# A trunk block on one core: block sums on token rows, and the MLP's second product in two groups of eight pairs

## The chip, the cores and the metric

The kernel runs on one core of a Trainium2 chip. The metric is the device time of one execution in microseconds. Before the change the median of three runs is 1608.74 us (1605.66 to 1609.58).

## The reference

One layer on 1024 frames of width 1024, all in float32: a mixing step (a convolution and a recurrent branch), a cross-attention into 256 memory tokens, and an MLP, each with a norm ahead and a residual add behind. The change concerns the end of the attention and the MLP:

```
hf = rmsnorm(x, g_ffn)                              # x: 1024 x 1024
x = x + square(relu(hf @ w_ff1)) @ w_ff2            # w_ff1: 1024 x 4096, w_ff2: 4096 x 1024
return rmsnorm(x, g_final)
```

## The kernel before, in words

**Precision.** Each float32 operand of a matmul is split into two parts, hi (a cast on ScalarE, L70) and lo (the value less hi, L71, on VectorE or, where a call says so, on GpSimd). A product is three matmuls: hi by hi, hi by lo, lo by hi (`mm3`, L79 to L81), added up in one PSUM bank of 128x512.

**Seven products instead of eight.** Both matrix products of the MLP are done on 2x2 blocks with seven block products and sums of blocks ahead and behind (j = 1 to 7). For `hf @ w_ff1` the token side is cut into two halves of 512 tokens and two halves of 512 features; the sums of these blocks are made once, in `blocks` (L1190), row block by row block (128 tokens). Row blocks 0 to 3 belong to the first token half and give b1 and b2 alone. Row blocks 4 to 7 give the other five, b3 to b7: the normed rows are transposed on TensorE, and sums are taken out of PSUM on VectorE and GpSimd.

**Up (the first product).** `up` (L1319) runs over 16 pairs of 128 columns of `w_ff1`, seven block products of 12 matmuls each. `up_operands` loads a pair's weights (L1290) and splits them, a pair ahead. A result is squared after relu on ScalarE (L1337, L1338), and the seven sums that the second product needs on its left are stored to `da` in memory (L1332), all from SyncE's queue; four of the seven come from sums on GpSimd.

**Down (the second product).** For each pair and j, a 128x512 left operand comes back from `da` (L1434) and a right one is a block, or a difference of blocks, of two rows of `w_ff2` (L1397, 512 KB a load). Before, the pairs stand in four groups of four. For a group and a j, four row blocks i are worked off one after the other: one bank, 12 matmuls for the four pairs, one drain into `acc[j, i]` (ScalarE copy L1454 in the first group, VectorE add L1456 later). The operands of the next j are prepared while this j runs, one pair per row block: the right lo part on VectorE, the left one on GpSimd (`down_operands`, L1400). Ahead of the first group's second row block 16 residual loads from `dx` are issued (`residual`, L1384). In the last group `merge` (L1461) adds the seven results up, half of them on VectorE and half on GpSimd, and `finish_rows` (L1486) does the final norm.

**What sets the order.** Each engine works off its own queue in order. A scheduler sets that order when the program is built, by a priority that is the place in the code (`self.at(p, ...)` gives code the priority of another place) and by an estimate of when inputs are ready. Waits between engines are semaphores, set by the data. Buffers are rings of a fixed number of tiles; a new use of a tile waits for the last reader of the old one. SyncE issues all loads and stores; an issue that waits holds up all behind it.

Of the kernel before, what the change touches and what calls it, by code (L numbers as in the profile page):

```python
# [25 lines left out]
GROUP = 4  # L26
GROUPS = PAIRS // GROUP
TAPS = 31
# [21 lines left out]
class Trunk:  # L50
# [189 lines left out]
    def norm(self, pool, src, g):  # L240
        t, r = self.rms_scale(pool, src)
        self.nc.vector.scalar_tensor_tensor(t, src, r, g, ALU.mult, ALU.mult)
        return t
# [25 lines left out]
    def run(self):  # L269
# [13 lines left out]
        with ctx:  # L283
# [46 lines left out]
            x1 = [px1.tile([P, D], F32, name=f"x1_{i}") for i in range(8)]  # L330
# [45 lines left out]
            B, feed = self.attention(pT, pQ, pG, pn, h1, x1, ahead, swap)  # L376
            early = tc.cur_priority
# [3 lines left out]
            self.mlp([push(right, n) for n in ("pE", "pF", "pS")], pn, B, early, lambda: (pop(left, 2), push(left, "pD"))[1])  # L381
            pop(right, 4)
# [697 lines left out]
    def attention(self, pT, pQ, pG, pn, h1, x1, ahead, swap):  # L1080
# [65 lines left out]
        def feed():  # L1146
            i, t = norms.pop(0)
            self.blocks(pT, t, i, B)
# [20 lines left out]
        return B, feed  # L1169
# [20 lines left out]
    def blocks(self, pool, t, i, B):  # L1190
# [4 lines left out]
        def turned(k):  # L1195
            pp = self.bank(self.ps, "mm")
            for j in range(4):
                nc.tensor.transpose(pp[:, j * P : (j + 1) * P], t[:, (k + j) * P : (k + j + 1) * P], self.ident)
            return pp.rearrange("p (k t) -> p k t", t=P)

        def at(p):
            return [z[:, :, ts_] for z in B[p]]

        def tmp():
            return pool.tile([P, 2, M], F32, tag="pe", name="tc", bufs=4).rearrange("p a (k t) -> p (a k) t", t=P)

        if i < 4:
            for p, k in ((1, 0), (2, 4)):
                self.split(*at(p), turned(k))
            return  # L1210
        pp = turned(0)
        b12 = tmp()
        nc.scalar.copy(b12, pp)
        hi, lo = at(1)
        t1 = tmp()
        nc.vector.tensor_tensor(t1, pp, f32(hi), ALU.subtract)
        nc.gpsimd.tensor_tensor(t1, t1, f32(lo), ALU.subtract)
        pp = turned(4)
        t2 = tmp()
        nc.vector.tensor_tensor(t2, pp, t1, ALU.subtract)  # L1220
        self.split(*at(6), t2)
        nc.vector.tensor_tensor(b12, pp, b12, ALU.subtract)
        self.split(*at(7), b12)
        self.split(*at(5), t1, nc.gpsimd)
        self.split(*at(3), pp)
        hi, lo = at(2)
        t4 = tmp()
        nc.vector.tensor_tensor(t4, f32(hi), t2, ALU.subtract)
        nc.gpsimd.tensor_tensor(t4, t4, f32(lo), ALU.add)
        self.split(*at(4), t4, nc.gpsimd)  # L1230
# [5 lines left out]
    def mlp(self, pools, pn, B, early, deeper):  # L1236
        (self.pE, self.pF, self.pS), self.pn = pools, pn
# [4 lines left out]
        def first():  # L1242
            for p in range(2):
                next(made[p])
                next(made[p])

        self.at(early, first)
# [5 lines left out]
        for u in ups:  # L1253
            for _ in u:
                pass
        self.down_tiles(deeper())
        stages = [(g, j) for g in range(GROUPS - 1) for j in (1, 5, 6, 7, 4, 2, 3)]
        stages += [(GROUPS - 1, j) for j in (1, 6, 7, 5, 4, 2, 3)]
        made = [[], []]
        for _ in self.down_operands(*stages[0], *made):  # L1260
            pass
        for n, (g, j) in enumerate(stages):
            now, made = made, [[], []]
            ahead = self.down_operands(*stages[n + 1], *made) if n + 1 < len(stages) else iter(())
            self.down(g, j, *now, ahead)
# [4 lines left out]
    def ring_of(self, *tags):  # L1270
        return itertools.cycle(
            [lambda a=a: a[0].tile(a[1], a[2], tag=a[3], name=a[3], bufs=a[4]) for a in tags for _ in range(a[4])]
        )

    def up_tiles(self):

        wide = [P, 2, HALF]
        self.operands = (self.pE, wide, F32R, "s", 6), (self.pS, wide, F32R, "s", 3)
        self.rows_of = (self.pm, [P, D], F32, "ms", 2), (self.pE, [P, D], F32, "w", 2)
        self.sring = self.ring_of(*self.operands)  # L1280

    def up_operands(self, p, out):
# [3 lines left out]
        for k in range(2):  # L1286
            pool, tag = ((self.pm, "ms"), (self.pE, "w"))[k]
            w = pool.tile([P, 4, 256], F32, tag=tag, name="w1", bufs=2)
# [30 lines left out]
    def up(self, p, A, B, ahead):  # L1319
# [11 lines left out]
        def put(j, z):  # L1331
            nc.sync.dma_start(self.da[j - 1, p], z)  # L1332
# [14 lines left out]
        c11 = put(1, act(product(2), p1))  # L1347
# [6 lines left out]
        c22 = put(4, act(pp, u3))  # L1354
# [4 lines left out]
        c21 = put(2, act(product(4), u3))  # L1359
        put(3, pooled(s2, c21, s2, ALU.subtract))  # L1360

    def down_tiles(self, pD):
# [16 lines left out]
        own = (pD, [P, 2, HALF], F32R, "r", 7), (pD, [P, D], F32, "w2", 8)  # L1379
        self.sring, self.wring = self.ring_of(own[0], *self.operands), self.ring_of(*self.rows_of, own[1])  # L1380
        self.rows = {}
        self.sums = lambda: sums(*((j, i) for j in (1, 5, 6, 7, 4, 2, 3) for i in range(4) if (j, i) not in self.acc))

    def residual(self):  # L1384

        nc, acc = self.nc, self.acc
        nc.sync.dma_start(self.gfin, self.a["g_final"].rearrange("(o d) -> o d", o=1).broadcast_to([P, D]))
        for j, o, c in ((5, 4, HALF), (4, 4, 0), (2, 0, 0), (3, 0, HALF)):
            for i in range(4):
                nc.sync.dma_start(acc[j, i], self.dx[i + o, :, c : c + HALF])  # L1390
        for i in range(4):
            self.both(acc[3, i], acc[3, i], acc[5, i], ALU.subtract, nc.gpsimd)

    def row(self, g, e, q):
        t = next(self.wring)()
        f = 2 * (g * GROUP + q) + e
        self.nc.sync.dma_start(t, self.a["w_ff2"][0, f * P : (f + 1) * P, :])  # L1397
        return t

    def down_operands(self, g, j, left, right):  # L1400

        nc, rows = self.nc, self.rows
        if (g, 0) not in rows:
            rows[g, 0] = [self.row(g, 0, q) for q in range(GROUP)]
        if j == 3 and g < GROUPS - 1:
            rows[g + 1, 0] = [self.row(g + 1, 0, q) for q in range(GROUP)]
        for q in range(GROUP):
            b11, b12 = (rows[g, 0][q][:, n * HALF : n * HALF + HALF] for n in range(2))
            if j not in (1, 5) or g == GROUPS - 1 and j == 5:
                b21, b22 = (rows[g, 1][q][:, n * HALF : n * HALF + HALF] for n in range(2))  # L1410
            if j == 1:
                t = b11
            elif j == 4:
                t = self.both(b11, b21, b11, ALU.subtract)
            elif j in (2, 3):
                t = b21 if j == 2 else b22
            elif g < GROUPS - 1:

                if j == 5:
                    t = self.both(b11, b12, b11, ALU.subtract)  # L1420
                elif j == 6:
                    t = self.both(b11, b22, b11, ALU.subtract)
                else:
                    t = self.both(b12, b22, b12, ALU.subtract)
            elif j == 6:

                self.both(b12, b22, b12, ALU.subtract)
                t = self.both(b11, b12, b11, ALU.add)
            elif j == 7:
                t = b12  # L1430
            else:
                t = self.both(b12, b22, b11, ALU.subtract)
            st = self.py_tile(F32)
            nc.sync.dma_start(st, self.da[j - 1, g * GROUP + q])  # L1434
            for out, src, eng in ((right, t, nc.vector), (left, st, nc.gpsimd)):
                z = next(self.sring)()
                self.split(z[:, 0], z[:, 1], src, eng)
                out.append((z[:, 0], z[:, 1]))
            if j == 1 and q == GROUP - 1:
                rows[g, 1] = [self.row(g, 1, q) for q in range(GROUP)]  # L1440
            yield

    def down(self, g, j, left, right, ahead):
        nc = self.nc
        for i in range(4):
            pp = self.bank(self.ps, "mm")
            ts_ = slice(i * P, i * P + P)
# [76 lines left out]
```

## Time and profile before

| | |
|---|---|
| median of 3 runs | 1608.74 us (1605.66 to 1609.58) |
| profiled execution | 1608.75 us, of it span 1607.0 us |
| TensorE busy | 1504.7 us, 94% |
| VectorE, ScalarE, GpSimd busy | 1225.4, 657.3, 676.6 us |
| bytes moved | 201.15 MB, mean 125 GB/s |
| granted TensorE clock, mean | 0.965 |

The span runs from the first to the last instruction of the profiled execution. "Busy" is the time in which an engine had an instruction of its own to work on; "PEclk" is the clock that TensorE was granted, 1.00 for 2.4 GHz and 0.50 for 1.2 GHz, as a mean over a stretch. In rows, `out<-in` names the tiles without their numbers, `xN` counts instructions, and a bracket at the end is how long the engine stood idle ahead of the row and what released it. All up to about 900 us (mixing, attention's queries and scores) is the same in both kernels. The up runs from about 939 to 1259 us, the down from 1266 us on.

### The profile page before, as it was taken

How to read it: one execution, taken by the hardware profiler on the slowest of the kernel's cores; microseconds unless marked ns; L12 is line 12 of the kernel's file. 1: busy time of each engine (PE TensorE's matmuls, PEld its weight loads, DVE VectorE, ACT ScalarE, POOL GpSimd, SP SyncE). 2: the span in 40 equal slices, each digit the busy share in tenths (PEclk: the TensorE clock that was granted, in tenths of full speed). 3: DMA queues.
4: the chain of work that ended last, by engine and by line, in shares of the span. 5: the costliest groups of instructions: out<-in, count | busy, mean ns of one | idle time of the engine just before them, and what ended most of it. 6: DMA issues, size and time to landing. Idle time of an engine off the chain costs nothing.

```text
span 1607.0 us, 22127 instructions
## 1 busy us (share of the span) xinstructions
PE 1504.7 (94%) x8066; PEld 1221.3 (76%) x8066; DVE 1225.4 (76%) x1691; ACT 657.3 (41%) x1219; POOL 676.6 (42%) x529
## 2 busy tenths in 40 slices
PE   6998988999999999999999949999999899999986
PEld 4776766778877778888888738888888678888864
DVE  5979898998888986473554788666655688899997
ACT  5423223223556452343222354555554354344323
POOL 4212337424345451421010075544444485565774
PEclk9999998989999999999999979999999999999997
DMA  7144436354344332231100314544444774544322
GB/s 236 41 152 137 125 105 187 99 165 127 110 126 135 122 119 73 79 98 45 49 14 27 132 39 151 171 144 148 160 151 164 255 269 144 158 146 148 93 59 105
DMA packets 171119, 201.15 MB, mean 125 GB/s; under 512 B 11679, under 2 KB 116439, under 8 KB 171010
## 3 DMA queue, kind: packets, MB, share of 16 engines
q1 hardware_dynamic: 171010, 199.73, 39.5%
q8 instruction: 64, 1.05, 0.3%
q14 instruction: 45, 0.37, 0.1%
HBM read 139.92 MB, written 59.77 MB: 124 GB/s over the span
## 4 chain that ended last, share of the span: by engine, by line
PE 66%; DVE 18%; issue 5%; DMA 5%; POOL 4%; ACT 2%; SPq 1%; DVEq 0%; POOLq 0%; ACTq 0%
DVE acc L617 7%; PE mm L80 5%; PE mm L79 5%; PE mm L81 5%; PE pr L80 5%; PE pr L81 5%; PE pr L79 5%; PE mm L445 3%; PE ep L81 2%; PE cp L81 2%; PE ep L80 2%; PE cp L80 2%; PE cp L79 2%; PE ep L79 2%; PE py L79 2%
## 5 line engine op out<-in xcount | busy, mean ns | idle before, releaser
L617 DVE SCALAR_TENSOR_TENSOR acc<-u,cw,acc 128x1024 f32<-128x1024 f32 (+1 forms) x150 | 205.1, 1367 | 3.8
L263 POOL TENSOR_TENSOR wlo<-wst,whi 128x1024 fp32r<-128x1024 f32 (+2 forms) x34 | 86.5, 2548 | 139.9 <-ACT whi L262 139.7
L71 POOL TENSOR_TENSOR s<-y,s 128x512 fp32r<-128x512 f32 x70 | 115.8, 1679 | 43.4 <-ACT s L70 39.0
L71 DVE TENSOR_TENSOR s<-f,s 128x512 fp32r<-128x512 f32 x48 | 53.3, 1112 | 52.9 <-ACT s L70 52.9
L93 POOL TENSOR_TENSOR rsr<-rsv,mhalf 128x1 f32<-128x1 f32 x34 | 20.1, 590 | 164.8 <-DVE rsv L88 161.1
L70 ACT CAST s<-w 128x512 fp32r<-128x512 f32 x92 | 56.7, 619 | 76.5 <-PE us L81 32.6
L71 POOL TENSOR_TENSOR r<-y,r 128x512 fp32r<-128x512 f32 x42 | 67.9, 1640 | 40.0 <-ACT r L70 40.0
L1337 ACT ACTIVATE y<-y 128x512 f32<-128x512 f32 x64 | 40.4, 632 | 79.6 <-DVE y L1233 72.0
L71 DVE TENSOR_TENSOR s<-w,s 128x512 fp32r<-128x512 f32 x58 | 64.4, 1123 | 10.3 <-ACT s L70 10.3
L1233 POOL TENSOR_TENSOR s<-y 128x512 f32<-128x512 f32 x32 | 41.5, 1317 | 59.8 <-ACT y L1338 59.8
L71 POOL TENSOR_TENSOR s<-w,s 128x512 fp32r<-128x512 f32 x34 | 46.3, 1366 | 37.6 <-ACT s L70 37.6
L445 PE MATMUL mm<-memT,wkv 128*128 128x256 f32 x256 | 61.3, 385 | 0.0
L71 DVE TENSOR_TENSOR r<-w,r 128x512 fp32r<-128x512 f32 x44 | 56.5, 1304 | 3.7 <-ACT r L70 3.7
L881 DVE TENSOR_TENSOR fs<-xt,PL 128x4 f32<-128x4 f32 (+15 forms) x128 | 53.9, 421 | 6.2 <-ACT PL L873 3.4
L262 ACT CAST whi<-wst 128x1024 fp32r<-128x1024 f32 (+2 forms) x34 | 35.0, 1031 | 56.9 <-PE mm L80 15.0
L1069 POOL TENSOR_TENSOR wql<-wst,wqh 128x1024 fp32r<-128x1024 f32 x8 | 20.0, 2495 | 88.6 <-ACT wqh L1068 88.6
L79 PE MATMUL mm<-hT1hi,whi 128*128 128x512 f32 (+1 forms) x120 | 50.9, 425 | 2.6 <-DVE z L501 1.4
L81 PE MATMUL mm<-hT1hi,wlo 128*128 128x512 f32 (+1 forms) x120 | 50.0, 416 | 2.7 <-POOL wlo L263 2.7
L445 PEld LDWEIGHTS mm<-memT,wkv 128*128 128x128 f32 x256 | 46.4, 190 | 6.1
L70 ACT CAST r<-w 128x512 fp32r<-128x512 f32 x44 | 27.2, 618 | 58.0 <-PE cp L81 40.9
L70 ACT CAST s<-f 128x512 fp32r<-128x512 f32 x64 | 38.3, 621 | 28.8 <-DVE f L1233 26.3
L80 PE MATMUL mm<-hT1lo,whi 128*128 128x512 f32 (+1 forms) x120 | 49.4, 411 | 0.0
(1002 smaller groups left out, 5030.6 us busy)
## 6 DMA issues: line engine op xcount, KB each, us to landing
w<-in_w_ff_dram SPq DMA_DIRECT2D x58, 512.0 KB
y<-da SPq DMA_DIRECT2D x112, 256.0 KB
da<-y SPq DMA_DIRECT2D x80, 256.0 KB
wst<-in_w_in_dram SPq DMA_DIRECT2D x32, 512.0 KB
da<-s SPq DMA_DIRECT2D x32, 256.0 KB
dz<-sg SPq DMA_DIRECT2D x24, 256.0 KB
dz<-z SPq DMA_DIRECT2D x24, 256.0 KB
xt<-in_x_dram SPq DMA_DIRECT2D x8, 512.0 KB
```

Source lines behind the costliest of these rows:

```text
L70: nc.scalar.copy(hi, src)
L71: (eng or nc.vector).tensor_tensor(lo, src, f32(hi), ALU.subtract)
L79: nc.tensor.matmul(ps, lh, rh, start=first and k == 0, stop=False)
L80: nc.tensor.matmul(ps, lh, rl, start=False, stop=False)
L81: nc.tensor.matmul(ps, ll, rh, start=False, stop=last and k == n - 1)
L262: nc.scalar.copy(hi, st)
L263: nc.gpsimd.tensor_tensor(lo, st, f32(hi), ALU.subtract)
L445: nc.tensor.matmul(dst, w[:, k, :], mem[k // 4][:, k % 4, :], start=k == 0, stop=k == KC - 1)
L617: nc.vector.scalar_tensor_tensor(acc, u[:, t : t + n], self.cw[:, t * 4 + c : t * 4 + c + 1], acc, ALU.mult, ALU.add)
L881: nc.vector.tensor_tensor(tmp, x, rows, ALU.mult)
L1233: (eng or self.nc.vector).tensor_tensor(out, x, y, op)
L1337: nc.scalar.activation(c, c, AF.Relu)
```

## The change

1. `GROUP` goes from 4 to 8. `down` now works in steps (group, j, pair): a step does its three matmuls on each of four open banks, and all four are drained after eight pairs. The last block (last group, j = 3) is done row block by row block, when all eight operands are there. Operands are prepared six steps ahead (`AHEAD`), the first six at the priority of the last up pair.
2. Rows of `w_ff2` are loaded as two halves of 256 KB, the second row of a pair only when the second j needs it. The residual loads are spread over four j, and the final gain is loaded in the last group.
3. Both lo parts of a step are made on VectorE; all merges on GpSimd. The final norm scales one half row early (`half_row`), and at the end takes one scale on VectorE and one on ScalarE (`rows_out`).
4. `blocks` takes the four sums of a row block on normed token rows (in place: GpSimd for row blocks 4 to 6, VectorE for 7), and then transposes and splits five blocks instead of two. For this the normed rows of blocks 0 to 3 stay in `x1`, and the store of a row to `dx` now stands ahead of its norm.
5. The stores of c11, c22 and c21, three of a pair's seven, go to ScalarE's queue. The rings of weights and operands turn in another order.

The core of the diff (other lines follow from these):

```diff
-GROUP = 4
+GROUP = 8
+AHEAD = 6
...
-                    norms.append((i, self.norm(pn, x1[i], g)))
                     nc.sync.dma_start(self.dx[i], x1[i])
+                    norms.append((i, self.norm(pn, x1[i], g, i < 4)))
...
+        def put(p, src):
             pp = self.bank(self.ps, "mm")
             for j in range(4):
+                nc.tensor.transpose(pp[:, j * P : (j + 1) * P], src[:, j * P : (j + 1) * P], self.ident)
+            hi, lo = (z[:, :, ts_] for z in B[p])
+            self.split(hi, lo, pp.rearrange("p (k t) -> p k t", t=P))
...
+        def less(out, x, y):
+            return self.both(out, x, y, ALU.subtract, nc.vector if i == 7 else nc.gpsimd)
...
+        (b11, b21), (b12, b22), (t1, t2) = (halves(z) for z in (x1[i - 4], t, x1[i]))
+        less(t1, b12, b11)
+        less(t2, b22, t1)
+        put(3, b22)
+        put(5, t1)
+        put(6, t2)
+        put(7, less(b12, b22, b12))
+        put(4, less(b21, b21, t2))
...
+        steps = [(g, j, q) for g in range(GROUPS) for j in ORDER[g] for q in range(GROUP)]
...
+        for n in range(AHEAD):
+            self.at(late, lambda: ahead(n))
+        for n, step in enumerate(steps):
+            ahead(n + AHEAD)
+            self.down(*step, ready)
...
-        c11 = put(1, act(product(2), p1))
+        c11 = put(1, act(product(2), p1), nc.scalar)
...
-        c22 = put(4, act(pp, u3))
+        c22 = put(4, act(pp, u3), nc.scalar)
...
-        c21 = put(2, act(product(4), u3))
+        c21 = put(2, act(product(4), u3), nc.scalar)
...
+    def row(self, g, q, e, n):
...
+        f, cs = 2 * (g * GROUP + q) + e, slice(n * HALF, n * HALF + HALF)
+        self.nc.sync.dma_start(self.rows[g, q, e][:, cs], self.a["w_ff2"][0, f * P : (f + 1) * P, cs])
...
-            for out, src, eng in ((right, t, nc.vector), (left, st, nc.gpsimd)):
...
-                self.split(z[:, 0], z[:, 1], src, eng)
+            self.split(z[:, 0], z[:, 1], src)
...
+            self.open = [self.bank(self.ps, "mm") for _ in range(4)]
...
+        def part(i, q, right, left):
+            ts_ = slice(i * P, i * P + P)
+            self.mm3(self.open[i], [(left[0][:, ts_], left[1][:, ts_])], [right], q == 0, q == GROUP - 1)
...
+        if not (last and j == 3):
+            now = ready.pop(0)
+            for i in range(4):
+                part(i, q, *now)
+        elif q == GROUP - 1:
+            for i in range(4):
+                for k in range(GROUP):
+                    part(i, k, *ready[k])
+                self.drain(g, j, i)
+            return
...
-        eng = nc.vector if i % 2 else nc.gpsimd
...
+            self.both(acc[to, i], acc[to, i], acc[by, i], ALU.add, nc.gpsimd)
```

**Where the order changes.** TensorE, from the last transposes to the first up product; `junk` is a normed row, `x1_k` a row block that the sums were taken in, `b1h` and `b1l` the parts of block 1. Before:

```order
L1198 MATMUL py_7885<-ident_115,junk_7821 128x128 x4
L1198 MATMUL us_7895<-ident_115,junk_7821 128x128 x4
L1198 MATMUL ep_7941<-ident_115,junk_7860 128x128 x4
L1198 MATMUL cp_7951<-ident_115,junk_7860 128x128 x4
L1198 MATMUL mm_7981<-ident_115,junk_7916 128x128 x4
L1198 MATMUL pr_7991<-ident_115,junk_7916 128x128 x4
L1198 MATMUL py_8012<-ident_115,junk_7972 128x128 x4
L1198 MATMUL us_8022<-ident_115,junk_7972 128x128 x4
L79 MATMUL mm_8074<-b1h_7471,s_8058 128x512
L80 MATMUL mm_8074<-b1l_7472,s_8058 128x512
```

After:

```order
L1212 MATMUL pr_7981<-ident_115,x1_1_3392 128x128 x4
L1212 MATMUL ep_7999<-ident_115,junk_7925 128x128 x4
L1212 MATMUL cp_8006<-ident_115,x1_6_3395 128x128 x4
L1212 MATMUL mm_8013<-ident_115,x1_6_3395 128x128 x4
L1212 MATMUL us_8038<-ident_115,junk_7989 128x128 x4
L1212 MATMUL pr_8021<-ident_115,junk_7925 128x128 x4
L1212 MATMUL mm_8045<-ident_115,x1_7_3397 128x128 x4
L1212 MATMUL py_8029<-ident_115,x1_2_3394 128x128 x4
L81 MATMUL mm_8106<-b1h_7471,s_8090 128x512
L82 MATMUL mm_8106<-b1l_7472,s_8090 128x512
L83 MATMUL mm_8106<-b1h_7471,s_8090 128x512
```

The two transposes per row block became five, of rows and of sums, and the first up product stands behind that of `x1_2`, the last sum of row block 6; three transposes of row block 7 follow it.

ScalarE, from the last squares of the up to the first casts of the down (`y` is a result or a loaded left operand, `ms` a row of `w_ff2`, `r` and `s` operands). Before:

```order
L1337 ACTIVATE y_10568<-y_10568 128x512
L1338 ACTIVATE y_10568<-y_10568 128x512
L1337 ACTIVATE y_10591<-y_10591 128x512
L1338 ACTIVATE y_10591<-y_10591 128x512
L70 CAST s_10647<-y_10642 128x512
L70 CAST r_10620<-ms_10610 128x512
L70 CAST r_10623<-y_10618 128x512
L70 CAST r_10628<-ms_10612 128x512
```

After:

```order
L1341 ACTIVATE y_10600<-y_10600 128x512
L1342 ACTIVATE y_10600<-y_10600 128x512
L1341 ACTIVATE y_10623<-y_10623 128x512
L1342 ACTIVATE y_10623<-y_10623 128x512
L1336 DMA da_62<-y_10623 128x512
L72 CAST s_10687<-y_10682 128x512
L72 CAST r_10651<-ms_10647 128x512
L72 CAST r_10654<-y_10649 128x512
L72 CAST r_10662<-ms_10658 128x512
```

The store of the last result (c21 of the last pair) now stands in ScalarE's queue, between its square and the first cast of the down.

GpSimd in the last group (`p60` is `acc[6, 0]`, and so on; `r` and `s` with `L71` are left lo parts). Before:

```order
L71 TENSOR_TENSOR r_12720<-y_12715,r_12720 128x512
L71 TENSOR_TENSOR s_12745<-y_12740,s_12745 128x512
L1233 TENSOR_TENSOR p60_10679<-p60_10679,p10_10671 128x512
L1233 TENSOR_TENSOR p20_10691<-p20_10691,p10_10671 128x512
L1233 TENSOR_TENSOR p62_10681<-p62_10681,p12_10673 128x512
L1233 TENSOR_TENSOR p22_10693<-p22_10693,p12_10673 128x512
L71 TENSOR_TENSOR s_12768<-y_12763,s_12768 128x512
L71 TENSOR_TENSOR s_12791<-y_12786,s_12791 128x512
L71 TENSOR_TENSOR s_12814<-y_12809,s_12814 128x512
L71 TENSOR_TENSOR s_12837<-y_12832,s_12837 128x512
L1233 TENSOR_TENSOR p70_10683<-p70_10683,p60_10679 128x512
L71 TENSOR_TENSOR r_12861<-y_12856,r_12861 128x512
```

After:

```order
L1236 TENSOR_TENSOR p60_10732<-p60_10732,p10_10724 128x512
L1236 TENSOR_TENSOR p20_10744<-p20_10744,p10_10724 128x512
L1236 TENSOR_TENSOR p61_10733<-p61_10733,p11_10725 128x512
L1236 TENSOR_TENSOR p21_10745<-p21_10745,p11_10725 128x512
L1236 TENSOR_TENSOR p62_10734<-p62_10734,p12_10726 128x512
L1236 TENSOR_TENSOR p22_10746<-p22_10746,p12_10726 128x512
L1236 TENSOR_TENSOR p63_10735<-p63_10735,p13_10727 128x512
L1236 TENSOR_TENSOR p23_10747<-p23_10747,p13_10727 128x512
L1236 TENSOR_TENSOR p70_10736<-p70_10736,p60_10732 128x512
L1236 TENSOR_TENSOR p71_10737<-p71_10737,p61_10733 128x512
```

Before, merges stand between lo parts for the next j; now merges stand alone, for all four row blocks, and the lo parts are in VectorE's queue.

## Rows read from the trace of the kernel before

**Rows 1.** The page, busy time and share of TensorE, TensorE's weight loads and the others.
```profile
PE 1504.7 (94%) x8066; PEld 1221.3 (76%) x8066; DVE 1225.4 (76%) x1691; ACT 657.3 (41%) x1219; POOL 676.6 (42%) x529
```

**Rows 2.** Table of stretches: window, length, busy of PE, PEld, DVE, ACT, POOL, clock, DMA share.
```profile
920.00:965.00 45.00, 22.24 (x96) 17.03 (x95) 37.61 (x45) 24.94 (x45) 33.29 (x25) 0.73 0.16 51
...
1000.00:1100.00 100.00, 100.00 (x443) 82.81 (x442) 66.78 (x83) 51.46 (x85) 51.52 (x39) 1.00 0.49 159
...
1245.00:1270.00 25.00, 18.25 (x73) 14.62 (x72) 9.29 (x10) 10.44 (x18) 10.10 (x9) 0.89 0.51 179
1270.00:1290.00 20.00, 15.82 (x65) 12.40 (x64) 14.85 (x18) 5.38 (x11) 9.90 (x8) 0.93 1.03 373
1290.00:1315.00 25.00, 24.29 (x96) 19.46 (x96) 24.81 (x18) 15.61 (x30) 24.57 (x16) 0.89 0.65 222
...
1400.00:1500.00 100.00, 100.00 (x443) 82.81 (x442) 86.27 (x94) 38.43 (x72) 60.08 (x38) 1.00 0.47 140
...
1540.00:1590.00 50.00, 43.73 (x170) 33.12 (x171) 46.87 (x54) 15.50 (x36) 36.47 (x25) 0.93 0.20 64
1590.00:1607.00 17.00, 3.67 (x17) 2.70 (x15) 10.06 (x22) 5.06 (x14) 2.20 (x4) 0.67 0.42 155
```

**Rows 3.** TensorE's timeline: start us, us, engine, line, operation, tiles, count, idle ahead.
```profile
908.57 0.60 PE L1198 MATMUL us<-ident,junk 128*128 128x128 f32 x4
...
962.98 0.79 PE L79 MATMUL py<-b5h,s 128*128 128x512 f32 x1 [12.61 <-ACT s L70]
...
1258.60 0.39 PE L80 MATMUL us<-b4l,s 128*128 128x512 f32 x1
1258.83 0.39 PE L81 MATMUL us<-b4h,s 128*128 128x512 f32 x1
1265.96 0.79 PE L79 MATMUL mm<-r 128*128 128x512 f32 x1 [6.75 <-ACT r L70]
...
1568.57 0.79 PE L81 MATMUL mm<-r 128*128 128x512 f32 x1 [4.06 <-POOL r L71]
...
1593.28 0.39 PE L81 MATMUL us<-s 128*128 128x512 f32 x1
```

**Rows 4.** GpSimd's timeline: two operations of the block sums, one stretch of the last group.
```profile
924.62 2.25 POOL L1217 TENSOR_TENSOR tc<-tc,b1l 128x512 f32<-128x512 f32 x1 [0.25 <-DVE tc L1216]
...
960.41 1.26 POOL L71 TENSOR_TENSOR b4l<-tc,b4h 128x512 fp32r<-128x512 f32 x1 [0.73 <-ACT b4h L70]
...
1566.81 3.39 POOL L71 TENSOR_TENSOR r<-y,r 128x512 fp32r<-128x512 f32 x2
```

**Rows 5.** GpSimd by lines from 920 to 965 us, the powers: busy, mean ns | idle.
```profile
L93 POOL TENSOR_TENSOR rsr<-rsv,mhalf 128x1 f32<-128x1 f32 x4 | 2.6, 660 | 7.4 <-DVE rsv L88 7.4
```

**Rows 6.** VectorE's timeline: norms, operations with GpSimd idle and busy, the end.
```profile
921.14 1.28 DVE L242 SCALAR_TENSOR_TENSOR junk<-x,rsr,g 128x1024 f32<-128x1024 f32 x1
...
933.93 1.60 DVE L242 SCALAR_TENSOR_TENSOR junk<-x,rsr,g 128x1024 f32<-128x1024 f32 x1
...
1282.28 1.28 DVE L1233 TENSOR_TENSOR w<-w,w 128x512 f32<-128x512 f32 x2
...
1567.32 3.43 DVE L1233 TENSOR_TENSOR p<-p,p 128x512 f32<-128x512 f32 x2
...
1599.38 0.68 DVE L1456 TENSOR_TENSOR p<-us,p 128x512 f32<-128x512 f32 x1
...
1602.60 1.41 DVE L1496 SCALAR_TENSOR_TENSOR p<-p,rsr,gfin 128x512 f32<-128x512 f32 x2 [0.73 <-POOL rsr L93]
```

**Rows 7.** ScalarE's timeline at the start of the down.
```profile
1264.25 0.62 ACT L70 CAST s<-y 128x512 fp32r<-128x512 f32 x1 [2.93 <-DMA y<-da]
```

**Rows 8.** SyncE's timeline of DMA issues at the end of the up.
```profile
1242.57 14.28 SPq L1332 DMA_DIRECT2D da<-y  x5
1256.94 0.88 SPq L1434 DMA_DIRECT2D y<-da  x2
```

**Rows 9.** DMA view from 1262 to 1292 us, totals.
```profile
DMA packets 5248, 11.07 MB, mean 369 GB/s; under 512 B 576, under 2 KB 576, under 8 KB 5247
```

More of the change, by code (lines that the diff above doesn't have):

```diff
@@ L380, in run, with deeper @@
             pop(right, 2)
[L381 to L382 removed]
+            def deeper():
+                pop(left, 2)
+                pop(right, 2)
+                return push(left, "pD"), push(right, "pR")
+            self.mlp([push(right, n) for n in ("pE", "pF", "pS")], pn, B, early, deeper)
+            pop(right, 3)
             pop(left, 3)
@@ L1240, in mlp @@
         made = [self.up_operands(p, A[p]) for p in range(PAIRS)] + [iter(())]
[L1242 to L1247, printed above, removed]
+        for p in range(2):
+            for _ in range(2):
+                self.at(early[p], lambda: next(made[p]))
         ups = [self.up(p, A[p], B, made[p + 1]) for p in range(PAIRS)]
@@ L1252, in mlp, with ahead @@
             pass
-        for u in ups:
-            for _ in u:
-                pass
[L1256 to L1265, printed above, removed]
+        for p in range(PAIRS):
+            late = tc.cur_priority
+            for _ in ups[p]:
+                pass
+        self.down_tiles(*deeper())
+        steps = [(g, j, q) for g in range(GROUPS) for j in ORDER[g] for q in range(GROUP)]
+        ready = []
+        def ahead(n):
+            if n < len(steps):
+                ready.append(self.down_operands(*steps[n]))
+        for n in range(AHEAD):
[3 more added lines that the diff above has]
+            self.down(*step, ready)
     def temp(self):
@@ L1443, in down @@
[L1443 to L1447, printed above, removed]
-            self.mm3(pp, [(h[:, ts_], l[:, ts_]) for h, l in left], right)
-            if g == i == 0 and j == 1:
-                self.sums()
-                self.residual()
-            t = self.acc[j, i]
-            if g == 0 and j in (1, 6, 7):
-                nc.scalar.copy(t, pp)
-            else:
-                nc.vector.tensor_tensor(t, pp, t, ALU.add)
-            if g == GROUPS - 1:
-                self.merge(j, i)
-            next(ahead, None)
+        wide, row = [P, 2, HALF], [P, D]
@@ new lines, in down @@
+    def down(self, g, j, q, ready):
+        nc, last = self.nc, g == GROUPS - 1
+        if q == 0:
+            if g == 0 and j == 1:
+                self.sums()
+                self.residual(5, 4, HALF)
+            elif g == 0 and j == 5:
+                self.residual(3, 0, HALF)
+            elif g == 0 and j == 6:
+                self.residual(4, 4, 0)
+            elif g == 0 and j == 7:
+                self.residual(2, 0, 0)
+            elif last and j == 1:
+                nc.sync.dma_start(self.gfin, self.a["g_final"].rearrange("(o d) -> o d", o=1).broadcast_to([P, D]))
+            self.open = [self.bank(self.ps, "mm") for _ in range(4)]
[4 more added lines that the diff above has]
+            now = ready.pop(0)
+            for i in range(4):
+                part(i, q, *now)
[5 more added lines that the diff above has]
+            return
+        if q == GROUP - 1:
+            for i in range(4):
+                self.drain(g, j, i)
@@ L1461, in merge, with drain @@
+    def drain(self, g, j, i):
+        nc, t, pp = self.nc, self.acc[j, i], self.open[i]
+        if g == 0 and j == 5:
+            self.both(self.acc[3, i], self.acc[3, i], t, ALU.subtract, nc.gpsimd)
+        if g == 0 and j in (1, 6, 7):
+            nc.scalar.copy(t, pp)
+        else:
+            nc.vector.tensor_tensor(t, pp, t, ALU.add)
+        if g == GROUPS - 1:
+            self.merge(j, i)
     def merge(self, j, i):
         nc, acc = self.nc, self.acc
-        eng = nc.vector if i % 2 else nc.gpsimd
```

213 lines of the change are left out of this document (100 added, 113 removed).

## Prediction

> **What bounds the kernel now.** I read first the page's busy shares: TensorE works 94% of the span [rows 1], so time can be won only where it idles or runs at its lower clock. The table of stretches says where that is [rows 2]. From 1000 to 1100 and from 1400 to 1500 us it is full at clock 1.00. In the stretches that this change touches are three holes: 920 to 965 (22.24 us busy of 45), 1245 to 1315 (58.36 of 70), and 1540 to the end (47.40 of 67). All three cost clock too: 0.73, 0.89 to 0.93, and 0.67 to 0.93.
>
> TensorE's timeline gives the pace: at full clock 128x512 matmuls start 0.23 us apart (1258.60 and 1258.83 [rows 3]); the listed 0.39 overlap. Each product of the MLP has 112 blocks of 12 such matmuls; at 0.2267 that is 304.7 us each, before and after alike.
>
> Hole A. The first up product that needs sums of token blocks (b5) starts at 962.98, after 12.61 us of idling [rows 3]. ScalarE is named, but GpSimd's own rows show what was slow: block sums and lo parts, 1.3 to 2.3 us each, the last at 960.41 [rows 4]. The norm that the first of these sums needs started at 921.14, the last norm ended at 935.5 [rows 6]. Four of the 112 blocks run inside the hole. The other 108 are worth 293.8 us, and 962.98 + 293.8 + 2.3 for some ten slow matmuls (0.43 us) is 1259.1, the end of this product: it loses nothing later.
>
> Hole B. Its last matmul starts at 1258.83; the second product's first starts at 1265.96, after 6.75 us of idling [rows 3]. ScalarE stood 2.93 us until 1264.25 for the load of a stored activation [rows 7]. That load was late on SyncE: five stores stand 14.28 us at the head of its queue, and loads follow from 1256.94 on [rows 8], with row loads and sixteen residual loads behind. From 1262 to 1292 the DMA engines move 369 GB/s [rows 9], with a share of 1.03 [rows 2]. Between 1259.06 and 1315 only 171 matmuls ran (65 + 96 in two stretches and ten before [rows 2]), worth 38.8 us of 55.9: 17 us lost.
>
> Hole C. The last matmul starts at 1593.28 and ends at about 1593.5 [rows 3]. From 1259.06 that is 334.4 us for 304.7 of work: 29.7 lost, 17 of it in B, 12.7 in the last stage. There GpSimd and VectorE both stream SBUF operations, and each then needs 1.7 us (pairs of 3.39 [rows 4] and 3.43 [rows 6]), while VectorE alone makes two in 1.28 [rows 6], 0.6 apiece as they are handed on. TensorE's longest wait there, 4.06 us, is for GpSimd's lo part [rows 3].
>
> The tail. From 1593.5 to the span's end at 1607.0 are 13.5 us. VectorE, in order behind the scales of other rows, drains the last bank only at 1599.38; the last two scales start at 1602.60 [rows 6].
>
> **The change part by part.** *Block sums* (A). Before, a block of the second token half was transposed, summed out of PSUM and split, with sums and lo parts on GpSimd; now four sums per row block are made on token rows, for three of the four row blocks on GpSimd, and then transposed. That adds 12 sets of four transposes, at most 0.6 us each [rows 3], nearly all inside the hole. What is late next is GpSimd's queue: in the order the first up product stands on TensorE behind the transposition of the last sum for x1_2. Until then GpSimd makes 12 sums, 3 lo parts of weights and three powers, and waits once for a norm (1.4 us, as 1.28 plus a handing over). Its mean operation in this stretch is 1.46 us: 33.29 us [rows 2] less four powers of 2.6 together [rows 5], over 21. Its first norm ends at 922.4 now; in the new order it stands ahead of three residual adds that it stands behind now, which I put at 919.2. So 919.2 + 15 x 1.46 + 3 x 0.6 + 1.4 = 944.3. With 1.26 each, the shortest [rows 4], it is 941; with 2.25, the longest, 956. I take 1.46, the mean of the place. The in-place norms of the first four rows now wait for their store to dx, and residual adds stand behind them on VectorE; a slip of some 5 us there is hidden before 944. Add 2.2 for slow matmuls and 1.3 for three transposes that follow: 944.3 + 304.7 + 3.5 = 1252.5 instead of 1259.1. Gain 6.6, bounds 10 and -5.
>
> *Stores from ScalarE* (B). Three of a pair's seven stores go to ScalarE's queue, right behind the squares that they store, so that the other stores and the loads don't wait for these squares at SyncE's head. No DMA of the trace is issued by ScalarE; I bound an issue by nothing and by SyncE's 0.44 (two in 0.88 [rows 8]): 48 are at most 21 us. ScalarE is 51% busy in this stage [rows 2], so they hide; one, 0.4, is on the path, ahead of the first down casts.
>
> *Second product in eights* (B, C). Operands are prepared six steps ahead, the first six in the last pair's time. Four banks stay open and change after three matmuls instead of twelve; the trace doesn't price that, and I take nothing (bounds 0 and 1% of 304.7, 3 us). Drains halve, off the path. At the start: an add 0.7, two activations 1.3, the issue 0.4, three casts 1.6: 4 us instead of 6.75. Then 2 us of slow matmuls as at 1265.96 and 1 of waits: 7 lost instead of 17. A step asks for 768 KB in 2.72 us, 289 GB/s, with the spread residual loads 337; the engines moved 369 [rows 9]. Gain 10; bounds 13 (only the 4 us) and 0 (the loads stay as full as now).
>
> Here a rule speaks against the change. The rows show 30 us of loads of 256 and 512 KB at 369 GB/s [rows 9]. The Trainium skill ("DMA: Bandwidth & Descriptors", Bandwidth) asks for batches of 1 MiB or more for 75% of peak, with 138 GB/s at 64 KB and 341 at 1 MB; row loads of 512 KB become halves of 256. By it B's gain would be near nothing; the rows, with many transfers in flight, don't bear it out.
>
> *Lo parts on VectorE, merges on GpSimd* (C). In the last group VectorE has 112 lo parts, 32 differences, 28 drains and some scales: 180 x 0.6 = 108 us beside TensorE's 152.4. GpSimd has 36 additions and gain products; each lasts 1.7 us beside VectorE and costs it 1.1 (one operation in 1.7 instead of 2.8): 40, together 148. That just fits, with operands some 16 us ahead; j=6 alone needs 24 us in 21.8. I take 3 us lost instead of 12.7, bounds 0 and 12.7. Gain 9.7. The first group has four merges and loses nothing.
>
> *Tail.* The last block goes row block by row block, so three of four rows are finished beside matmuls; one half row is scaled early, and one of the two last scales is ScalarE's. After the last matmul stand a drain 0.7, squares 0.7, a sum 0.15, a power 0.6, a scale 0.7 and 0.6 of handing over, 3.5; behind the scale the 3.0 from 1604.0 to the end, as now. 6.5 us instead of 13.5: gain 7, bounds 8 and 0 (VectorE again behind other rows).
>
> Sum: 6.6 + 10 + 9.7 + 7 = 33. The profiled execution took 1608.75 (span 1607.0), the median is 1608.74: 1576. All bounds at their best (10, 13, 12.7, 8) give 1565, all at their worst 1617.
>
> **The rivals.** (a) VectorE becomes the bound of the last group. For: 148 of 152 us, and each engine holds the other up [rows 4, 6]. Against: the lo parts leave GpSimd, where they were dearer. From 1400 to 1500 VectorE was busy for 86 us and bound nothing [rows 2]; if 90% is all that it gets to between its waits, 148 us take 165, 13 more than TensorE's: C stays, 1586. The Trainium skill ("SBUF — State Buffer", Who interferes with whom) says that a VectorE instruction with two SBUF inputs contends with a GpSimd one that reads SBUF, by an exclusive lock. The pairs of 3.39 and 3.43 agree.
>
> (b) The down's start stays bound by loads. For: the engines are full there now [rows 2], and half rows stand behind stores on SyncE. Against: the residual loads are spread. B gains nothing: 1586.
>
> (c) The block sums don't do it: TensorE stands in order behind transposes whose sums GpSimd makes one by one, between lo parts for two pairs. At 2.25 each, or with the first pairs' operands late, the start is at 956 to 963: A gives nothing or loses 5, 1583 to 1588.
>
> (d) Slower: ScalarE is held at its own stores. SyncE stood 14.28 us over five stores [rows 8], 2.9 each; if ScalarE stands so at three a pair, the casts of the next pair come late, and TensorE waits in every pair of 19 us. It decides from 33/16 = 2.1 us a pair. At 4 us a pair it costs 64: 1640. Against: behind the square that it stores, a store has nothing left to wait for but an older transfer.
>
> **How the numbers follow.** Forecast 0.52, (a) 0.2, (b) 0.1, (c) 0.1, (d) 0.08. The forecast's own range is 1566 to 1585. For 8 in 10 I take 1565 to 1596, which takes in (a) to (c) one at a time and leaves (d) and two rivals together. A difference of 0.3% (5 us) is about what can be told from none: faster 0.88; same 0.05, from (a) to (c) together or a mild (d); slower 0.07, from (d).
>
> **What would show it.** In the profile after: GpSimd's sum for x1_2 at about 944 and TensorE full from there; no wait for ScalarE's casts within the up product; the first down matmul 4 us after the up's last, and TensorE full 5 us later; a DMA share under 0.95 there; few waits for VectorE's lo parts in the last 150 us; 6.5 us of tail. A start of the up after 956, or over 8 us of idling in the last group, makes that term wrong; waits for casts in every pair make the sign wrong.

## The result and the profile after

The changed kernel takes 1572.78 us (median of four runs, 1570.75 to 1574.0) beside 1609.16 before: a ratio of 0.9777 (95% interval 0.9758 to 0.9795). 1576 was forecast, with 1565 to 1596 for the range. By the medians that is a gain of 36.4 us. The profiled execution is the fastest of the four: it took 1570.75, its span is 1569.0, 38.0 us less than before.

The table of stretches of the changed kernel, columns as in [rows 2]:

```profile
920.00:965.00 45.00, 36.76 (x174) 28.96 (x175) 37.43 (x50) 23.73 (x44) 28.72 (x21) 0.85 0.27 89
...
1000.00:1100.00 100.00, 100.00 (x443) 82.81 (x442) 63.85 (x82) 53.66 (x88) 49.74 (x39) 1.00 0.49 159
...
1245.00:1260.00 15.00, 10.78 (x36) 8.35 (x35) 8.02 (x13) 8.05 (x14) 5.33 (x5) 0.77 0.59 207
1260.00:1280.00 20.00, 20.00 (x90) 16.58 (x89) 17.19 (x29) 10.05 (x19) 0.00 (x0) 1.00 1.04 380
1280.00:1300.00 20.00, 20.00 (x89) 16.54 (x89) 19.61 (x27) 10.04 (x20) 14.08 (x4) 1.00 1.02 371
...
1400.00:1500.00 100.00, 100.00 (x443) 82.84 (x442) 87.46 (x120) 44.17 (x78) 28.14 (x18) 1.00 0.33 96
1500.00:1550.00 50.00, 50.00 (x222) 41.27 (x221) 44.62 (x59) 26.90 (x58) 34.39 (x24) 1.00 0.31 99
1550.00:1569.00 19.00, 11.83 (x52) 9.34 (x50) 4.97 (x9) 4.34 (x9) 1.62 (x3) 0.95 0.30 110
```

Hole C is gone: TensorE has no wait from 1260 to the end of its work. Holes A and B are shorter. TensorE's timeline gives their new ends:

```profile
943.19 0.48 PE L81 MATMUL mm<-b1h,s 128*128 128x512 f32 x1
943.51 0.40 PE L82 MATMUL mm<-b1l,s 128*128 128x512 f32 x1
...
1249.18 0.39 PE L83 MATMUL cp<-b4h,s 128*128 128x512 f32 x1
1253.79 0.79 PE L81 MATMUL mm<-r 128*128 128x512 f32 x1 [4.22 <-ACT r L72]
...
1561.44 0.39 PE L83 MATMUL cp<-w,r 128*128 128x512 f32 x1
```

Against [rows 3] the four terms of the profiled execution can be read off. The up ends at 1249.41 instead of 1259.06: 9.65 us. From there to the last matmul's end at 1561.67 are 312.3 us for 304.7 of work. All 7.6 lost lie in B, since the wait of 4.22 is TensorE's only one behind the up: B gains 9.4 (17 before), C 12.7. The tail is 7.3 us instead of 13.5: 6.2. Together 38.0.

GpSimd's timeline in hole A (it answers to [rows 4]): the first sum, two lo parts of weights between the sums, the power that these held up, and the last sum for x1_2.

```profile
917.40 1.27 POOL L1236 TENSOR_TENSOR x<-junk,x 128x512 f32<-128x512 f32 x1 [1.98 <-ACT b2h L72]
...
930.13 2.52 POOL L73 TENSOR_TENSOR s<-ms,s 128x512 fp32r<-128x512 f32 x2
...
933.83 0.54 POOL L95 TENSOR_TENSOR rsr<-rsv,mhalf 128x1 f32<-128x1 f32 x1
...
941.00 1.73 POOL L1236 TENSOR_TENSOR x<-x,x 128x512 f32<-128x512 f32 x1
```

It ends at 942.73, and the first up product follows at 943.19, behind that sum's transposes.

At the seam, ScalarE and SyncE (against [rows 7] and [rows 8]):

```profile
1251.71 0.33 ACTq L1336 DMA_DIRECT2D da<-y  x1
1252.08 0.62 ACT L72 CAST s<-y 128x512 fp32r<-128x512 f32 x1 [0.40 <-ACT y L1342]
```

```profile
1233.88 3.84 SPq L1336 DMA_DIRECT2D da<-y  x2
1237.81 2.56 SPq L1440 DMA_DIRECT2D y<-da  x4
```

Four loads of stored activations are issued from 1237.81, almost 12 us before the up ends (before: from 1256.94, 2 us before its end). Ahead of the down's first casts ScalarE no longer waits for a load; only its squares, its own issue of 0.33 us and its order stand there.

### The profile page after: what moved, and what is told of

It is laid out like the page before. It is cut to its first block, busy times and chain, and to the rows that moved or that the text cites. A ratio compares the mean times of both kernels' runs of the same rounds, so it can differ in the third digit from the quotient of the medians.

```text
span 1569.0 us, 22055 instructions
## 1 busy us (share of the span) xinstructions
PE 1496.6 (95%) x8114; PEld 1220.9 (78%) x8114; DVE 1168.3 (74%) x1721; ACT 665.6 (42%) x1223; POOL 533.1 (34%) x435
## 5 line engine op out<-in xcount | busy, mean ns | idle before, releaser
L1236 POOL TENSOR_TENSOR p<-p,p 128x512 f32<-128x512 f32 x32 | 60.9, 1932 | 197.8 <-DVE p L1495 174.1
L73 DVE TENSOR_TENSOR s<-y,s 128x512 fp32r<-128x512 f32 x57 | 44.9, 790 | 22.8 <-ACT s L72 22.8
L95 POOL TENSOR_TENSOR rsr<-rsv,mhalf 128x1 f32<-128x1 f32 x26 | 15.2, 585 | 137.1 <-DVE rsv L90 133.5
L72 ACT CAST s<-y 128x512 fp32r<-128x512 f32 x57 | 35.2, 621 | 58.2 <-PE us L83 26.8
L72 ACT CAST r<-y 128x512 fp32r<-128x512 f32 x55 | 33.8, 620 | 55.7 <-PE cp L83 23.2
L73 DVE TENSOR_TENSOR r<-y,r 128x512 fp32r<-128x512 f32 x55 | 42.8, 782 | 13.7 <-ACT r L72 13.7
L72 ACT CAST s<-w 128x512 fp32r<-128x512 f32 x69 | 42.6, 619 | 21.8 <-DMA w<-in_w_ff_dram 6.9
L892 DVE TENSOR_REDUCE xt<-fs 128x2 f32<-128x4 f32 (+15 forms) x128 | 45.2, 353 | 3.1
```

The costliest lines, as they stand in the source:

```text
L72: nc.scalar.copy(hi, src)
L73: (eng or nc.vector).tensor_tensor(lo, src, f32(hi), ALU.subtract)
L892: nc.vector.tensor_reduce(xt[:, 0:m, 2 * k : 2 * k + 2], tmp, AX.X, ALU.add)
L1236: (eng or self.nc.vector).tensor_tensor(out, x, y, op)
```

## The experiments

All are changes of the changed kernel. Ratios are to the kernel before, in runs on the same chip. Differences in microseconds are between medians of different chips, where the kernel before took 1606.65 to 1609.16; by the ratios they come out up to 2.5 us larger or smaller.

**Stores back on SyncE.**

```diff
-        c11 = put(1, act(product(2), p1), nc.scalar)
+        c11 = put(1, act(product(2), p1))
```

(likewise c22 and c21)

> The changed kernel (1572.8 us) with the stores of c11, c22 and c21 back on SyncE; all else as changed. Theory (the stores on SyncE stand in front of the loads of stored activations): in the new order the first such load then stands behind the store of the last pair's c22, whose square ends about 1 us before the up's last matmul, so the operands of the down's first step land some 2 us later than ScalarE is ready for them; the first down matmul comes 6 to 9 us after the up's last instead of 4.4, and the time is 1574 to 1578. Rival (issuing engines share the same transfers, so only issue time moves): 1572 to 1573.5, and the hole stays at 4.4 us.

1574.89 us, ratio 0.9802 (0.9786 to 0.9818). SyncE's and ScalarE's timelines:

```profile
1234.62 14.28 SPq L1336 DMA_DIRECT2D da<-y  x5
1248.95 1.86 SPq L1440 DMA_DIRECT2D y<-da  x4
```

```profile
1254.39 0.62 ACT L72 CAST s<-y 128x512 fp32r<-128x512 f32 x1 [1.01 <-DMA y<-da]
```

The same 14.28 us stand at SyncE's head, and the loads go out 11 us later, as the theory said (9 us later by the up's end, which is 1.7 later here). ScalarE then waits only 1.01 us, because its own squares stand ahead of the cast anyway; TensorE's wait is 4.83 instead of 4.22, not the forecast 6 to 9. The time lies in the theory's range, but the two intervals overlap: the stores are worth 0.6 us by the trace, 2 by the medians and some 4 by the ratios, and the times alone can't tell that from nothing.

**All residual loads at once.**

```diff
-                self.residual(5, 4, HALF)
...
+                for z in ((5, 4, HALF), (3, 0, HALF), (4, 4, 0), (2, 0, 0)):
+                    self.residual(*z)
```

> The changed kernel with all 16 residual loads (4 MB) issued in the first block of the down, as before, instead of over four blocks; in the order 12 of them (3 MB, 8 us at 380 GB/s) then stand ahead of row loads of steps 5 to 8. Theory (the DMA engines are full from 1255 to 1300, and the loads are hidden only because the residual is spread): TensorE waits 4 to 8 us in the first block, 1577 to 1581. Rival (six steps of lookahead cover it): 1572 to 1574, no wait over 0.5 us.

1579.29 us, ratio 0.9831 (0.9816 to 0.9846). TensorE's timeline has one new wait:

```profile
1282.16 0.80 PE L81 MATMUL mm<-s,r 128*128 128x512 f32 x1 [6.58 <-ACT r L72]
```

The theory holds: 6.58 us of wait, 6.5 by the medians. SyncE's 16 issues take 10.44 us from 1264.21 on, and a load of rows of `w_ff2` goes out behind them at 1275.02; ScalarE's casts wait 11.0 us for such a load, until 1280.45. The 16 loads also go out before 1300 in the changed kernel; only their place in the queue differs.

**Two steps of lookahead.**

```diff
-AHEAD = 6
+AHEAD = 2
```

> The changed kernel (1572.8 us) with operands prepared two steps ahead instead of six. Theory (in the last group VectorE is full for over 60 us, 1444 to 1530, and gets by on the 16 us of lead): with 5.4 us of lead TensorE waits there for VectorE's lo parts, 3 to 10 us, and loses 1 to 5 more at the down's start, where fewer steps are loaded ahead: 1577 to 1587. Rival (six is far more than is needed): 1572 to 1574, no wait over 0.5 us behind the first down matmul.

1575.13 us, ratio 0.9805 (0.9786 to 0.9825). The waits of TensorE from 1240 us on are one row:

```profile
PE mm L81 <- ACT r L72: 6.5, 1, 6.5
```

The theory falls for the last group: VectorE is as full there (134.1 us of the 152 from 1400 on, 132.8 in the changed kernel), and 5.4 us of lead are enough. What six steps buy is 2.3 us at the start of the down, by this one trace; the intervals of the two kernels overlap, so the times don't confirm it.

**Left lo parts back on GpSimd.**

```diff
-            self.split(z[:, 0], z[:, 1], src)
+            self.split(z[:, 0], z[:, 1], src, nc.gpsimd if src is st else None)
```

> The changed kernel with the left lo parts of the down back on GpSimd; merges stay on GpSimd, right lo parts on VectorE. Theory (GpSimd was the dear place, 1.3 to 1.7 us an operation): in the last group GpSimd has 56 lo parts and 36 merges at about 1.6 us, 147 us with waits for drains and casts in line, beside 152.4 us of TensorE; TensorE waits for GpSimd's lo parts there, 3 to 12 us in all, 1576 to 1585. Rival (VectorE is the tight engine of the last group, full from 1444 to 1530, so relief for it helps or does nothing): 1571 to 1573, no wait for GpSimd.

1590.26 us, ratio 0.9898 (0.9883 to 0.9913): 17.5 us over the changed kernel, more than forecast. TensorE's waits behind the up:

```profile
PE mm L83 <- POOL s L73: 8.6, 2, 7.4
PE mm L81 <- ACT r L72: 4.2, 1, 4.2
PE mm L83 <- POOL r L73: 3.8, 1, 3.8
PE mm L82 <- DVE s L73: 2.2, 3, 1.5
```

8.6 us are in the last group, as said; 3.8 and the 2.2 are in the first 65 us of the down, which the forecast had left out.

**Merges on VectorE.**

```diff
-            self.both(acc[to, i], acc[to, i], acc[by, i], ALU.add, nc.gpsimd)
+            self.both(acc[to, i], acc[to, i], acc[by, i], ALU.add)
```

> The changed kernel with the merges of the last group on VectorE instead of GpSimd (the gain products of the early half rows stay on GpSimd). Theory (a merge on GpSimd costs VectorE about 1.1 us by holding it up, its own only 0.6): VectorE's busy time from 1400 to 1552 us, now 132.8, falls by 10 to 18 us although it does 28 operations more; the time stays 1571 to 1574, as TensorE has no wait there to lose. Rival (VectorE is the bound of that group, so any operation more on it shows): VectorE's busy time rises by 17 us and TensorE waits, 1576 to 1585.

1572.34 us, ratio 0.9780 (0.9762 to 0.9798): the same. The last group in the table of stretches, first of the changed kernel, then of this one:

```profile
1400.00:1552.00 152.00, 152.00 (x671) 125.75 (x670) 132.77 (x179) 71.45 (x137) 62.53 (x41) 1.00 0.33 99
```

```profile
1400.00:1552.00 152.00, 152.00 (x672) 125.65 (x671) 123.12 (x204) 72.36 (x138) 19.87 (x14) 1.00 0.32 97
```

VectorE does 25 operations more in 9.65 us less, GpSimd 27 fewer. So, as an estimate, a merge on GpSimd costs VectorE about (9.65 + 25 x 0.6) / 27 = 0.9 us against 0.6 of its own. TensorE has nothing to gain from it.

**Four groups of four.**

```diff
-GROUP = 8
-ORDER = ((1, 5, 6, 7, 4, 2, 3), (1, 6, 7, 5, 4, 2, 3))
+GROUP = 4
+ORDER = 3 * ((1, 5, 6, 7, 4, 2, 3),) + ((1, 6, 7, 5, 4, 2, 3),)
```

> The changed kernel with four groups of four pairs instead of two of eight; steps, four open banks, lookahead, stores, sums, spread loads and engines as changed (56 drains more). Theory (the last group has to hold the 36 merges and gain products, whatever its length): VectorE then needs about 100 x 0.6 + 36 x 1.1 = 100 us there in 76 us of TensorE, less 16 us of lead, and TensorE waits 6 to 12 us; 1579 to 1586. Rival (the group's size is nothing by itself, the gain is from engines and loads): 1572 to 1575.

1581.32 us, ratio 0.9839 (0.9824 to 0.9854). The range is right, the place is not. GpSimd's and TensorE's timelines at the end:

```profile
1546.25 8.91 POOL L1236 TENSOR_TENSOR p<-p,p 128x512 f32<-128x512 f32 x6
1555.10 3.84 POOL L1236 TENSOR_TENSOR p<-p,gfin 128x512 f32<-128x512 f32 x3
```

```profile
1563.17 0.40 PE L83 MATMUL cp<-w,s 128*128 128x512 f32 x1
```

TensorE ends at 1563.4, 1.7 us after the changed kernel's, with 1.8 us of waits. But GpSimd's merges, in 76 us instead of 152, run on to 1559, the row norms behind them come late, and the tail is 16.4 us of the span of 1579.8 instead of 7.3.

**Block sums as before.** The method `blocks` and the norm of the kernel before, in the changed kernel.

```diff
-                    norms.append((i, self.norm(pn, x1[i], g, i < 4)))
+                    norms.append((i, self.norm(pn, x1[i], g)))
```

> The changed kernel with block sums as before (transposes first, sums out of PSUM, lo parts of two blocks on GpSimd); the rest as changed. Theory (the sums on token rows shorten the chain through GpSimd): the hole from 920 to 963 comes back, the up ends 8 to 11 us later, 1581 to 1584. Rival (in-order TensorE behind one-by-one sums gives no gain of its own; the gain of 9.7 us at the up's end comes from the early operands of the first two pairs): 1573 to 1576.

1583.81 us, ratio 0.9860 (0.9843 to 0.9876), 11.0 over the changed kernel; the last up matmul starts at 1259.10, nearly where it was before. TensorE's timeline:

```profile
957.90 0.79 PE L81 MATMUL mm<-b1h,s 128*128 128x512 f32 x1 [10.13 <-ACT s L72]
...
1263.71 0.79 PE L81 MATMUL mm<-r 128*128 128x512 f32 x1 [4.22 <-ACT r L72]
```

The sums carry all of A's gain; the seam behind is the same 4.22.

**One row block's sums moved to VectorE.**

```diff
-            return self.both(out, x, y, ALU.subtract, nc.vector if i == 7 else nc.gpsimd)
+            return self.both(out, x, y, ALU.subtract, nc.vector if i > 5 else nc.gpsimd)
```

> The changed kernel with the token-row sums of row block 6 on VectorE as well (GpSimd keeps row blocks 4 and 5). Theory (GpSimd's chain of sums sets the start of the up, 943.2 now): four operations leave its end, the last sum that the first up product stands behind is then row block 7's, and the start comes 1 to 3 us earlier, 1570 to 1572. Rival (VectorE is 97% busy from 920 to 933 and the norms and lo parts of the same rows are in its queue, so the chain only changes engine): the start is at 943 or later, 1572 to 1576.

1577.44 us, ratio 0.9813 (0.9798 to 0.9828): slower by 4.7. From GpSimd's first sum to the first up product are 26.9 us (919.87 to 946.73) instead of 25.8, and a wait is new:

```profile
955.87 0.50 PE L81 MATMUL py<-b1h,s 128*128 128x512 f32 x1 [2.95 <-ACT s L72]
```

The rival holds: the work only changes engine, and the second pair's operands come late.

**The last square on VectorE.**

```diff
+            if not own:
+                nc.vector.scalar_tensor_tensor(c, c, 0.0, c, ALU.max, ALU.mult)
+                return c
...
-        c21 = put(2, act(product(4), u3), nc.scalar)
+        c21 = put(2, act(product(4), u3, p < PAIRS - 1), nc.scalar if p < PAIRS - 1 else nc.sync)
```

> The changed kernel in which relu and square of the last pair's c21 are one VectorE instruction (max with 0, times itself) and its store goes to SyncE, so that ScalarE's first down casts have nothing ahead of them. Theory (the 4.4 us between the products are the last result's add, two activations, the issue and three casts in line on ScalarE): the casts start 0.2 us after the up's last matmul, the first down matmul comes 1.4 to 2 us after it, and with the shorter idling fewer matmuls run at the lower clock: 1567 to 1570.5. Rival (the hole is the wait for stored activations and tiles, not ScalarE's queue): 1572 to 1574, the hole stays over 4 us.

1570.75 us, ratio 0.9760 (0.9743 to 0.9776). TensorE's timeline:

```profile
1254.61 0.50 PE L81 MATMUL mm<-r 128*128 128x512 f32 x1 [0.94 <-ACT r L72]
...
1258.49 0.80 PE L82 MATMUL mm<-r 128*128 128x512 f32 x1 [2.68 <-DVE r L73]
```

The wait for ScalarE is 0.94, so most of the hole was its queue. Most of it comes back at a lo part, which stands on VectorE behind the square (1.67 us) and another lo part (1.75). The intervals overlap: by time alone this is not settled.

**Both: last square on VectorE, and operands of the first steps in tiles that come free earlier.**

```diff
-        self.sring = self.ring_of((pD, wide, F32R, "r", 7), (self.pE, wide, F32R, "s", 6), (pR, wide, F32R, "s", 2))
+        self.sring = self.ring_of((self.pE, wide, F32R, "s", 6), (pD, wide, F32R, "r", 7), (pR, wide, F32R, "s", 2))
```

> As the run with VectorE's last square, and the ring of the down's operands begins with tiles whose last reader is an up product of the last pair, instead of tiles that lie where the block sums lay until the last matmul; both casts of the first step can then be made before the up ends. Theory (the rest of the hole is the wait for that place): at most 0.7 us between the products, no matmuls at the lower clock there, 5.5 to 7.5 us less than the changed kernel: 1565 to 1567.5. Rival (lo parts on VectorE, behind the last add and square, hold TensorE at its ninth matmul instead): the same 2 us are lost there, 1567 to 1570.

1567.94 us, ratio 0.9748 (0.9731 to 0.9765): 4.8 us under the changed kernel. The intervals of the ratios just overlap, but the slowest run here (1569.7) is below the fastest of the changed kernel (1570.75). TensorE's and VectorE's timelines:

```profile
1249.56 0.39 PE L83 MATMUL cp<-b4h,s 128*128 128x512 f32 x1
1249.85 0.50 PE L81 MATMUL mm<-s 128*128 128x512 f32 x1
...
1254.18 0.50 PE L83 MATMUL mm<-s 128*128 128x512 f32 x1 [2.22 <-DVE s L73]
```

```profile
1250.77 1.69 DVE L1342 SCALAR_TENSOR_TENSOR y<-y 128x512 f32<-128x512 f32 x1
1252.38 1.75 DVE L73 TENSOR_TENSOR s<-y,s 128x512 fp32r<-128x512 f32 x1
```

The first down matmul starts 0.06 us after the up's last one ends, and none runs at the lower clock (granted 1.00 from 1249 to 1263). The rival is right about the rest: 2.22 us for a lo part, both operations at 1.7 beside GpSimd.

**That square on GpSimd instead.**

```diff
-                nc.vector.scalar_tensor_tensor(c, c, 0.0, c, ALU.max, ALU.mult)
+                nc.gpsimd.tensor_scalar(c, c, 0.0, None, ALU.max)
+                nc.gpsimd.tensor_tensor(c, c, c, ALU.mult)
```

> As the run with both, but relu and square of the last c21 are two GpSimd instructions instead of one on VectorE, so that VectorE's queue has the first step's lo part right behind the last add. Theory (in the run with both, TensorE's 2.2 us are the last square of 1.69 us ahead of that lo part on VectorE): the wait falls to under 1 us, 1 to 2 us less than the run with both, 1565 to 1567. Rival (GpSimd streams three operations more just there, and a VectorE lo part beside it takes 1.75 instead of 0.68): the wait stays at 1.5 to 2.5 us, 1567 to 1569.

1567.72 us, ratio 0.9751 (0.9733 to 0.9769). TensorE's waits behind the up:

```profile
PE mm L81 <- ACT s L72: 1.2, 1, 1.2
PE mm L82 <- DVE s L73: 0.6, 1, 0.6
PE mm L83 <- DVE s L73: 0.6, 1, 0.6
```

The wait falls to 0.6, and two others come up instead, 2.4 us in all: no difference to the run with both. By their medians these two are the fastest versions.

**Early lo parts on VectorE** (on top of the run with both).

```diff
-        put(1, a11, nc.gpsimd if p < 2 else None)
-        put(2, a12, nc.gpsimd)
+        put(1, a11)
+        put(2, a12, nc.gpsimd if p > 1 else None)
```

> As the run with both, and the lo parts of products 1 and 2 of the first two pairs on VectorE instead of GpSimd, where three of them stand between the block sums (1.7, 2.5 us). Theory (GpSimd's chain sets the start of the up): the last sum for x1_2 ends 1 to 3 us earlier than at 942.7, and the time is 1 to 3 us under the run with both. Rival (as with the sums of row block 6, VectorE is full there and only passes the delay on through norms and lo parts): the same or up to 3 us more.

1572.97 us, ratio 0.9778 (0.9762 to 0.9794): 5 us slower than with both. VectorE's timeline:

```profile
930.34 3.43 DVE L73 TENSOR_TENSOR s<-ms,s 128x512 fp32r<-128x512 f32 x2
...
936.57 0.14 DVE L90 TENSOR_SCALAR rsv<-ssq 128x1 f32<-128x1 f32 x1
```

The two lo parts take 1.7 each beside GpSimd's sums and stand ahead of the scale of the seventh row's norm. From the first sum to the last are 27.2 us (920.76 to 947.92) instead of 25.3. The rival holds again. Counted from the first sum to the end of the span, this trace is 3.6 us longer than that of the run with both; the rest of the 5 us isn't explained by it.

## Why the prediction was right, and where it was not

The sum of 33 us came to 38.0 in the profiled execution and to 36.4 by the medians. A and C each gave 3 us more than was said, B and the tail up to 1 us less.

*Block sums.* Right in mechanism and place: 943.19 for 944.3, the chain of sums on GpSimd, the transposes behind. The run with old sums loses 11.0 us again. The gain is 9.65 where 6.6 was said: 1.1 is the earlier start, and the term that was mis-sized is the 2.2 us of slow matmuls, of which 0.2 came. TensorE had transposes to do until 943.19, with waits of 2.7 us at most, and its matmuls then start at full pace, 0.32 and 0.23 us apart. Part of that is luck: in the traces with the stores back, with the left lo parts on GpSimd and with four groups, some four matmuls there still run at half pace, and the up takes up to 1 us longer.

*Stores from ScalarE.* The issue costs 0.33 (bounds 0 and 0.44), and no wait for ScalarE arises in the up. That SyncE's head held the loads up is shown, but little of B's 9.4 us is seen to hang on it: 0.6 by the trace, and the times don't settle more. What carries B is above all the place of the residual loads (6.5 us); the lookahead's 2.3 stand in one trace only. No run loads whole rows of `w_ff2` again, so what the half loads are worth is open.

*Second product in eights.* The seam was worked out at 4 us and took 4.4; no wait follows it. "A DMA share under 0.95" there is the step that failed: it is 1.04 and 1.02 up to 1300. The 289 to 337 GB/s were what steps use, but SyncE issues ahead as far as tiles are free. Full DMA engines were not the bound; which load stood first was. So rival (b) named the right resource, but not what decides. As in the prediction, the rule of the Trainium skill ("DMA: Bandwidth & Descriptors", Bandwidth) on transfers of 1 MiB isn't borne out where many transfers are in flight: with loads of 256 KB the engines moved 380 and 371 GB/s.

*Lo parts and merges.* The 12.7 us are gone whole; 3 were left in the sum. GpSimd's lo parts were the cause: with the left ones put back TensorE waits for GpSimd again, and they cost 17.5 us, while the merges cost TensorE nothing on either engine. VectorE was busy for 132.8 of the 152 us from 1400 to 1552 where 148 were worked out, and a merge costs it about 0.9, not 1.1. The 16 us of lead that were to save the group weren't needed. Rival (a) is refuted. An operation with two SBUF inputs beside GpSimd took 1.7 us on VectorE, as [rows 6] had it. The Trainium skill's rule ("SBUF — State Buffer", Who interferes with whom) on two such inputs agrees.

*Tail.* 7.3 us for 6.5. The run with four groups shows one thing that it rests on: merges that are done before the last row block. No run takes back the early half row or ScalarE's scale, so their shares aren't shown.

*Rival (d)* shows nowhere: from 1000 to 1240 us TensorE has no wait at all. *Rival (c)* did not happen, but its condition is near: both attempts to lighten GpSimd's chain made the start later, by 1.1 and 2.2 us counted from the first sum.

## What to carry to other kernels

Look at a seam between two products as a queue problem: what stands in each in-order queue between the last result and the first operand, and which tiles the first operands must wait for. Filling the queues of DMA to the brim did no harm here, as long as the transfer that is needed first stood first. Before work goes from GpSimd to VectorE, check what else VectorE has in that stretch: in the down it had room, and moving the left lo parts was worth 17.5 us; at the start of the up it was full, and moving lo parts there lost 5.

## What was not expected of the hardware

A VectorE operation that reads PSUM and SBUF kept its 0.68 us while GpSimd streamed; one with two SBUF inputs took 1.75. The changed kernel's VectorE timeline has both within 2 us, with GpSimd busy from 926.78 to 932.61:

```profile
927.29 1.75 DVE L1236 TENSOR_TENSOR f<-ms 128x512 f32<-128x512 f32 x1
928.96 0.68 DVE L73 TENSOR_TENSOR b7l<-pr,b7h 128x512 fp32r<-128x512 f32 x1
```

Transposes alone brought TensorE's clock back. From 923.15 to 943.19 us it did nothing else. Its granted clock was 0.50 from 935 to 941, behind waits of up to 2.7 us, and 1.00 from 943 on: four transposes took 1.12 us at 941.10, but 0.66 at 942.78, ahead of the first up product.

The sum of GpSimd that starts hole A begins between 916.41 and 921.49 us in the profiled executions with the new sums, although the instructions ahead of it are the same; the runs of the kernel before differ by up to 7 us on one chip. So waits of one profile were compared here only from a point within it, and times by their intervals. Counted from that sum to the end of the span, the changed kernel takes 651.6 us; 652.2 with the stores back, 653.1 with two steps of lookahead, 651.1 with the last square on VectorE, 647.4 with both and 648.4 with that square on GpSimd. Each of these is a single execution.
